# Convolution sublayer of a six-sublayer encoder: the taps' diagonal blocks are made during the feed-forward sublayer ahead of it, kept in DRAM and loaded per channel tile; taps stand amid projection tiles; weight splits are held at the convolution's head

## Chip, cores and metric

The kernel runs on one core of a Trainium2 chip. The metric is device time in microseconds of one execution, lower is better. PE is the matmul engine, DVE the vector engine, ACT the scalar engine, POOL the general-purpose engine (GpSimd), SP the engine that here issues nearly every transfer.

## What is computed

Two layers of an encoder over 256 positions and 1024 channels, all in float32. A layer is a half-weight feed-forward sublayer, a mixer, and a second half-weight feed-forward sublayer. The mixer of the first layer is a convolution module, that of the second differential attention. In the kernel the six sublayers are called a (feed-forward), b (convolution), c, d (feed-forward), e (attention), f (feed-forward). The change touches a and b:

```python
def _half_ffn(x, g_pre, g_post, w_gate, w_up, w_down):        # a, c, d, f
    h = _rmsnorm(x, g_pre)
    f = (jax.nn.silu(h @ w_gate) * (h @ w_up)) @ w_down        # 1024 -> 2816 -> 1024
    return x + 0.5 * _rmsnorm(f, g_post)

def _conformer_conv(h, w_pw1, b_pw1, w_dw, b_dw, ln_g, ln_b, w_pw2, b_pw2):   # b
    u = h @ w_pw1 + b_pw1
    u = u[..., :D_MODEL] * jax.nn.sigmoid(u[..., D_MODEL:])
    c = depthwise_conv(u, w_dw, width=31, centred) + b_dw      # one filter per channel
    c = jax.nn.silu(_layernorm(c, ln_g, ln_b))
    return c @ w_pw2 + b_pw2
```

## The kernel before, in words

**Split products.** Each weight block of 128 x 1024 values is a job with a number. SP loads it into a `raw` buffer, ACT rounds it into `wh`, DVE writes the rest into `wl` (`split_to`), and PE forms three products per pair of operands: high by high, low by high, high by low (lines 176 to 178). Five `raw` buffers turn round (`NRAW`), so the load of job n waits for the split of job n-5. `pump` issues loads and splits up to a limit; `hold(first, n)` sets that limit to job first+n, and `release` lifts it or moves it on once the instructions given to it are done.

**Sublayer a.** `ffn` goes through 22 steps `kt`. Each step is a projection tile `gua` of 48 matmuls (gate and up), an evacuation on DVE and ACT (`sga`, `hfa`, then the split pair `hha`, `hla`), and 12 matmuls of the down projection into `acca`, which use the `hha` and `hla` of the step before. PSUM has two banks for `gua`, so the tile of step kt+2 cannot start before `hfa` of step kt has been written. After the last step `conv_params` (line 590) loads the convolution's taps and biases (one transfer of 31 rows, four small ones), turns them on PE (`pp`), and splits the taps into `wdh` and `wdl`, one scalar per channel and tap.

**Sublayer b.** `lead` makes channel tiles 0 to 3 (`pxb`, turned by `py`), `projs` tiles 4 to 7 (`gub`). `glu` turns each into `u`, split into `us` (high and low). Per channel tile ct, `build(ct)` makes two blocks `dg` of 128 x 1024 on DVE, in which each channel's 32 taps stand on diagonals (line 634), and `taps(ct)` multiplies them with `us` on PE in 96 matmuls of 32 rows (line 649) into four PSUM banks `cv`. Each bank is then folded: ACT copies half of it (`ca`, line 655), DVE adds (`ta`, line 656), ACT copies (`ca`, line 657), DVE adds into `co` (line 658). `centre` shifts and squares `co`. `step(ct)` is build(ct+1), taps, centre; the dictionary at the end of `conv` says after which tile's `glu` which steps stand. The layer norm's sums, `m2`, and the Silu into `zf` and `z` follow, then the second pointwise product `accb`.

**Order.** Each engine runs its instructions in the order of its row. The framework's scheduler fixes these rows when the kernel is built, from priorities and its own estimates; an instruction at the head of a row that waits holds everything behind it on that engine. `heads` names, for each sublayer, the job up to which loads and splits are held at its end (`None` for no hold); `LEAD` is 8.

Of the kernel before, what the change touches and what calls it, by code (L numbers as in the profile page):

```python
# [9 lines left out]
F32 = mybir.dt.float32  # L10
# [32 lines left out]
WARM0 = 6  # L43

# [10 lines left out]
def trunk_kernel(  # L55
# [289 lines left out]

    def hook_flips():
        while flips:
            tc.keep_in_program_order(T.transpose(*flips.pop(0), ident))
# [34 lines left out]
    def proj(w1, w2, f, name):  # L383
# [3 lines left out]
        for n, w in enumerate((w1, w2)):  # L387
            for k in range(KD):
                hi, lo = w(k)
                mm3(ps[:, n, :], hi[:, c], lo[:, c], xTh[:, k, :], xTl[:, k, :], k == 0, k == KD - 1)  # L390
                if (n, k) == (0, KD - 1):
                    hook_flips()
        return ps
# [99 lines left out]
    def ffn(hp, jb, name, late=None):  # L493
# [27 lines left out]
        for kt, ps in projs([(c, jb[c][:2]) for c in range(2, len(jb))], name):  # L521
            c, f = divmod(kt, 2)
            if kt == 4:
# [93 lines left out]

    def conv(hp, name):
# [11 lines left out]
        def build(ct):  # L630

            dgs[ct] = [big(f"dg{ct}{n}", F32R) for n in range(2)]
            for dg, w in zip(dgs[ct], (wdh, wdl)):
                V.tensor_tensor(dg.rearrange("p (t c) -> p t c", c=STRIP),
                                same.unsqueeze(1).to_broadcast([P, TAPS, STRIP]),
                                r32(w)[:, ct, :].unsqueeze(2).to_broadcast([P, TAPS, STRIP]), ALU.mult)

        def taps(ct):
# [6 lines left out]
            for j in range(TAPS // NPH):  # L645
                for n, (d, u) in enumerate(((dh, uh), (dl, uh), (dh, ul))):
# [13 lines left out]
        def centre(ct):  # L660
            c = co[ct]
            V.scalar_tensor_tensor(c, c, par[:, 16 + ct:17 + ct], shift, ALU.add, ALU.subtract)
            sqs[ct] = hp.tile([P, S], F32, tag="sq", name=f"sq{ct}", bufs=2)
            A.activation(sqs[ct], c, AF.Square)

        def lead():
            tm = [big(f"tm{tb}", F32).rearrange("p (i c) -> p i c", c=2 * FC) for tb in range(NTB)]
            for tb, i, ps in proj_x(JC1[:2], TWO, name):
                A.copy(tm[tb][:, i, :], ps)
                if tb == 0:  # L670
                    continue
                for f in range(2):
                    ps = ps_mi.tile([P, 2, S], F32, tag="mi", name=f"py{i}{f}")
                    for n in range(2):
                        for b in range(NTB):
                            T.transpose(ps[:, n, b * P:(b + 1) * P],
                                        tm[b][:, i, n * FC + f * P:n * FC + (f + 1) * P], ident)
# [47 lines left out]
        hold(J01[0][0].ids[0], 0)  # L725
        build(0)
        for ct, ps in lead():
# [12 lines left out]
            for n in {2: (0,), 3: (1,), 4: (2, 3), 5: (4,), 6: (5,), 7: (6, 7)}.get(ct, ()):  # L740
                step(n)
        A.activation(warm, par[:, 0:1], AF.Silu)
# [66 lines left out]
    def attn(hp, name):  # L809
# [115 lines left out]
        ("a", lambda p: ffn(p, J00, "a", late), ffn_norm_pre[0, 0], ffn_norm_post[0, 0], True, conv_params),  # L925
# [8 lines left out]
    heads = [None] + [jb[0][0].ids[0] for jb in (J01, J10)] + [None, J11[0][0].ids[0]]  # L934
# [52 lines left out]
```

## Time and profile before

| what | value |
|---|---|
| median of three runs | 1037.87 us (1035.88 to 1038.41) |
| the profiled execution | 1037.48 us |
| its span, first to last instruction | 1035.7 us |
| PE busy | 1010.0 us, 98% of the span |
| DVE busy | 653.1 us, 63% |
| ACT busy | 538.0 us, 52% |
| POOL busy | 50.7 us, 5% |
| transfers | 177.14 MB, of which 1.05 MB written |

The profile is of one execution. Its own time is 0.39 us under the median, and 1.8 us of it lie outside the span. The busy time of PE counts a matmul until its modelled end, so full busy time is not full speed; the granted clock of PE stands beside it as a share of 2.4 GHz. A line number belongs to the kernel before; in the kernel after, the same code stands some lines lower (L455 for L450, L545 for L538, L679 for L656).

### The profile page before, as it was taken

The numbers are of one execution on the slowest core, as the hardware profiler recorded it, in microseconds if no ns is written. First come the engines' busy times: TensorE is split into PE (matmuls) and PEld (weight loads), VectorE is DVE, ScalarE is ACT, GpSimd is POOL, SyncE is SP. The second block draws the span as 40 slices with busy tenths as digits, with TensorE's granted clock in tenths as the row PEclk, the third lists the DMA queues.
The fourth block names the chain that finished last, engine by engine and source line by source line (L and its number), as shares of the span: only waits on it lengthen the run. The fifth ranks groups of instructions, "written<-read, shape, count | busy, mean of one in ns | idle before, by whom it ended". The sixth has DMA issues, their size and how long they took to land.

```text
span 1035.7 us, 18641 instructions
## 1 busy us (share of the span) xinstructions
PE 1010.0 (98%) x7576; PEld 932.5 (90%) x7576; DVE 653.1 (63%) x993; ACT 538.0 (52%) x877; POOL 50.7 (5%) x92
## 2 busy tenths in 40 slices
PE   8999999988989999999999999999999999999997
PEld 7999999888887989999899999998899789999995
DVE  5775667688777584646477646556778667645542
ACT  6654544465457373535346535445578556535431
POOL 0000000031410000000000000001000100000000
PEclk9999999999899999999999999999999999999999
DMA  7887555371220585655537756563752237765511
GB/s 244 278 280 227 172 184 193 116 247 48 84 83 11 184 294 184 193 174 184 162 122 251 239 181 196 182 198 123 258 163 84 80 103 233 238 200 171 186 51 41
DMA packets 130366, 177.14 MB, mean 171 GB/s; under 512 B 6165, under 2 KB 112709, under 8 KB 130280
## 3 DMA queue, kind: packets, MB, share of 16 engines
q1 hardware_dynamic: 130280, 175.95, 52.8%
q8 instruction: 59, 0.97, 0.4%
q14 instruction: 27, 0.22, 0.1%
HBM read 174.88 MB, written 1.05 MB: 170 GB/s over the span
## 4 chain that ended last, share of the span: by engine, by line
PE 86%; DVE 5%; ACT 3%; issue 2%; DMA 1%; POOL 1%; SPq 0%; DVEq 0%; POOLq 0%; ACTq 0%
PE guf L177 3%; PE guc L177 3%; PE guc L176 3%; PE gua L177 3%; PE gud L178 3%; PE gud L176 3%; PE gua L178 3%; PE gua L176 3%; PE guf L176 3%; PE gud L177 3%; PE guf L178 3%; PE guc L178 3%; PE pxa L429 2%; PE cv L649 2%; PE accf L177 2%
## 5 line engine op out<-in xcount | busy, mean ns | idle before, releaser
L450 DVE TENSOR_TENSOR wl<-raw,wh 128x1024 fp32r<-128x1024 f32 x314 | 380.9, 1225 | 101.6 <-ACT wh L450 98.5
L450 ACT CAST wh<-raw 128x1024 fp32r<-128x1024 f32 x314 | 325.7, 1051 | 107.8 <-PE guc L177 11.6
L176 PE MATMUL gud<-xTh,wh 128*128 128x256 f32 x288 | 81.0, 281 | 0.0
L176 PE MATMUL gua<-xTh,wh 128*128 128x256 f32 x288 | 81.0, 281 | 0.0
L176 PE MATMUL guf<-xTh,wh 128*128 128x256 f32 x288 | 81.0, 281 | 0.0
L176 PE MATMUL guc<-xTh,wh 128*128 128x256 f32 x288 | 81.0, 281 | 0.0
L177 PE MATMUL gua<-xTl,wh 128*128 128x256 f32 x288 | 80.9, 281 | 0.0
L177 PE MATMUL guc<-xTl,wh 128*128 128x256 f32 x288 | 80.9, 281 | 0.0
L177 PE MATMUL guf<-xTl,wh 128*128 128x256 f32 x288 | 80.9, 281 | 0.0
L177 PE MATMUL gud<-xTl,wh 128*128 128x256 f32 x288 | 80.9, 281 | 0.0
L178 PE MATMUL guf<-xTh,wl 128*128 128x256 f32 x288 | 80.9, 281 | 0.0
L178 PE MATMUL guc<-xTh,wl 128*128 128x256 f32 x288 | 80.9, 281 | 0.0
L178 PE MATMUL gua<-xTh,wl 128*128 128x256 f32 x288 | 80.9, 281 | 0.0
L178 PE MATMUL gud<-xTh,wl 128*128 128x256 f32 x288 | 80.9, 281 | 0.0
L176 PEld LDWEIGHTS guf<-xTh,wh 128*128 128x128 f32 x288 | 54.3, 189 | 0.5
L176 PEld LDWEIGHTS guc<-xTh,wh 128*128 128x128 f32 x288 | 54.3, 189 | 0.5
L176 PEld LDWEIGHTS gud<-xTh,wh 128*128 128x128 f32 x288 | 54.3, 189 | 0.5
L176 PEld LDWEIGHTS gua<-xTh,wh 128*128 128x128 f32 x288 | 54.3, 189 | 0.5
L177 PEld LDWEIGHTS gud<-xTl,wh 128*128 128x128 f32 x288 | 54.3, 189 | 0.5
L177 PEld LDWEIGHTS guc<-xTl,wh 128*128 128x128 f32 x288 | 54.3, 188 | 0.5
L177 PEld LDWEIGHTS guf<-xTl,wh 128*128 128x128 f32 x288 | 54.3, 188 | 0.5
L177 PEld LDWEIGHTS gua<-xTl,wh 128*128 128x128 f32 x288 | 54.3, 188 | 0.5
(371 smaller groups left out, 2508.8 us busy)
## 6 DMA issues: line engine op xcount, KB each, us to landing
raw<-in_ffn_w_gate_dram SPq DMA_DIRECT2D x88, 512.0 KB, 4.9
raw<-in_ffn_w_up_dram SPq DMA_DIRECT2D x88, 512.0 KB, 5.0
raw<-in_ffn_w_down_dram SPq DMA_DIRECT2D x88, 512.0 KB, 4.7
raw<-in_conv_w_pw_dram SPq DMA_DIRECT2D x24, 512.0 KB, 4.6
raw<-in_attn_w_qkv_dram SPq DMA_DIRECT2D x24, 512.0 KB, 5.3
raw<-in_attn_w_o_dram SPq DMA_DIRECT2D x8, 512.0 KB, 4.3
gpre<-in_ffn_norm_pre_dram SPq DMA_DIRECT2D x3, 512.0 KB
x<-in_x_dram SPq DMA_DIRECT2D x2, 512.0 KB, 3.4
```

The lines of the kernel that those rows point to most:

```text
L176: T.matmul(o, sh, mh, start=first, stop=False)
L177: T.matmul(o, sh, ml, start=False, stop=False)
L178: T.matmul(o, sl, mh, start=False, stop=last)
L429: pin(T.matmul(ps[:, m * FC:(m + 1) * FC], s[:, k, c], w(k)[v], start=n + k == 0, stop=n == 2 and k == KD - 1))
L450: return A.copy(hi, src), V.tensor_tensor(lo, src, r32(hi), ALU.subtract)
L649: T.matmul(bank[r][:, 0:N], d[q, j * P:(j + 1) * P], u[q, NPH * j:NPH * j + N], start=j + n == 0, stop=(j, n) == (TAPS // NPH - 1, 2))
```

## The change

- `conv_params` runs inside sublayer a, at step 5, in place of its end. `diagonals`, called at each step of a, then makes the 16 blocks that `build` made before (now called `dm`, two buffers of 512 KB in turn), one per step in program order. Each is written to a DRAM buffer `kept` by a transfer that POOL issues, 512 KB each, 8.4 MB in all.
- `build(ct)` loads two blocks from `kept` by SP in place of making them on DVE.
- `taps` takes its 96 matmuls in the order high by high, high by low, low by high, each over all eight tap groups; before, the three stood together per tap group.
- step(1) and step(4) stand amid a projection tile (`mids`, run after its first 24 matmuls); step(0) stands after tile 2, step(2) after tile 4, step(3) after 5, step(5) after 6, steps 6 and 7 after 7.
- Splits are held at the end of a to the first eight jobs of the convolution and released by the lead's copies `tm`. At the end of b, `hold` is gone from the start of conv, and `centre(7)` releases the next splits on.
- The copies `tm` are grouped by i in place of tb.

```diff
+DIAG0 = 5
@@ proj
                 if (n, k) == (0, KD - 1):
                     hook_flips()
+                    while mids:
+                        mids.pop(0)()
@@ ffn
+            if aside is not None:
+                aside(hp, kt)
@@
+    def diagonals(hp, kt):
+        if kt == DIAG0:
+            with after(fetched[LATER]):
+                conv_params()
+        ct, n = divmod(kt - DIAG0 - 1, 2)
+        if kt <= DIAG0 or ct >= KD:
+            return
+        dg = hp.tile([P, 1024], F32R, tag="dg", name=f"dm{ct}{n}", bufs=2)
+        V.tensor_tensor(dg.rearrange("p (t c) -> p t c", c=STRIP),
+                        same.unsqueeze(1).to_broadcast([P, TAPS, STRIP]),
+                        r32((wdh, wdl)[n])[:, ct, :].unsqueeze(2).to_broadcast([P, TAPS, STRIP]), ALU.mult)
+        kept[ct, n] = dram.tile([P, 1024], F32, name=f"kept{ct}{n}")
+        G.dma_start(kept[ct, n], r32(dg))
@@ build
-            for dg, w in zip(dgs[ct], (wdh, wdl)):
-                V.tensor_tensor(dg.rearrange("p (t c) -> p t c", c=STRIP),
...
+            for n in range(2):
+                nc.sync.dma_start(r32(dgs[ct][n]), kept[ct, n])
@@ taps
-            for j in range(TAPS // NPH):
-                for n, (d, u) in enumerate(((dh, uh), (dl, uh), (dh, ul))):
+            for n, (d, u) in enumerate(((dh, uh), (dh, ul), (dl, uh))):
+                for j in range(TAPS // NPH):
@@ centre
+            if ct == KD - 1:
+                release(J01[0][0].ids[0], *done)
@@ lead
+            for m, (tb, i, ps) in enumerate(proj_x(JC1[:2], TWO, name)):
+                release((j0 + LEAD, j0 + LEAD + 2, j0 + LEAD + 4, j1 + 6)[m], A.copy(tm[i][:, tb, :], ps))
@@ conv
-        hold(J01[0][0].ids[0], 0)
-            for n in {2: (0,), 3: (1,), 4: (2, 3), 5: (4,), 6: (5,), 7: (6, 7)}.get(ct, ()):
+            for n in {2: (0,), 4: (2,), 5: (3,), 6: (5,), 7: (6, 7)}.get(ct, ()):
                 step(n)
+            mids.extend({3: [lambda: step(1)], 5: [lambda: step(4)]}.get(ct, []))
@@ subs, heads
-        ("a", lambda p: ffn(p, J00, "a", late), ffn_norm_pre[0, 0], ffn_norm_post[0, 0], True, conv_params),
+        ("a", lambda p: ffn(p, J00, "a", late, diagonals), ffn_norm_pre[0, 0], ffn_norm_post[0, 0], True, None),
-    heads = [None] + [jb[0][0].ids[0] for jb in (J01, J10)] + [None, J11[0][0].ids[0]]
+    heads = [jb[0][0].ids[0] for jb in (JC1, J01, J10)] + [None, J11[0][0].ids[0]]
```

What the rows look like after, at three places. In the names, the number behind the last underscore is the buffer's.

**PE, sublayer a, the down matmuls after the tile of step 5.** Before (`acca11` is the last of the four accumulators):

```order
L176 MATMUL acca11_537<-wh16_512,hha2_610 128x512
L177 MATMUL acca11_537<-wl16_513,hha2_610 128x512
L178 MATMUL acca11_537<-wh16_512,hla2_611 128x512
L176 MATMUL gua6_785<-xTh_99,wh18_524 128x256
L177 MATMUL gua6_785<-xTl_100,wh18_524 128x256
```

After:

```order
L177 MATMUL acca11_539<-wh16_514,hha2_612 128x512
L612 MATMUL pp_771<-ident_79,wdw_r_764 128x31 x8
L178 MATMUL acca11_539<-wl16_515,hha2_612 128x512
L179 MATMUL acca11_539<-wh16_514,hla2_613 128x512
L177 MATMUL gua6_817<-xTh_99,wh18_526 128x256
```

The eight transposes of the taps `wdw_r`, which stood at the end of a, now stand among these matmuls; the transpose of `par_r` follows ten matmuls into `gua6`.

**DVE, sublayer a, steps 9 and 10.** Before:

```order
L450 TENSOR_TENSOR wl39_1108<-raw39_1105,wh39_1107 128x1024
L538 TENSOR_TENSOR sga9_1111<-gua9_1038,row_602 128x256
L805 TENSOR_SCALAR lam_106<-le0_8203,le1_8211 128x1
L540 TENSOR_TENSOR sga9_1111<-sga9_1111,row_602 128x256
L542 TENSOR_TENSOR hfa9_1115<-gua9_1038,sga9_1111 128x256
L450 TENSOR_TENSOR wl40_1134<-raw40_1131,wh40_1133 128x1024
L450 TENSOR_TENSOR hla4_1017<-hfa9_1115,hha4_1016 128x256
L538 TENSOR_TENSOR sga10_1186<-gua10_1137,row_602 128x256
```

After:

```order
L455 TENSOR_TENSOR wl39_1152<-raw39_1149,wh39_1151 128x1024
L545 TENSOR_TENSOR sga9_1159<-gua9_1082,row_604 128x256
L638 TENSOR_TENSOR dm50_1768<-same_105,wdh_103 128x1024
L455 TENSOR_TENSOR wl40_1182<-raw40_1179,wh40_1181 128x1024
L638 TENSOR_TENSOR dm51_1855<-same_105,wdl_104 128x1024
L547 TENSOR_TENSOR sga9_1159<-sga9_1159,row_604 128x256
L828 TENSOR_REDUCE le1_8277<-lp1_8275 128x1
L549 TENSOR_TENSOR hfa9_1163<-gua9_1082,sga9_1159 128x256
L833 TENSOR_SCALAR subg_109<-subg_109 128x1
L638 TENSOR_TENSOR dm60_1916<-same_105,wdh_103 128x1024
L545 TENSOR_TENSOR sga10_1238<-gua10_1185,row_604 128x256
L455 TENSOR_TENSOR hla4_1061<-hfa9_1163,hha4_1060 128x256
```

Three builds now stand between `sga9` and `hla4`, the evacuation of step 9. All 16 builds stand in DVE's row between the evacuations of steps 5 and 11; each but the first two waits for the write of the build two places ahead of it. On PE the first four matmuls of `gua11` stand ahead of the 12 down matmuls after `gua10`.

**ACT, sublayer b, ahead of the first fold of channel tile 0.** Before:

```order
L450 CAST wh83_2587<-raw83_2585 128x1024
L450 CAST us00_2527<-u0_2529 128x256
L450 CAST us10_2544<-u1_2546 128x256
L450 CAST wh84_2617<-raw84_2615 128x1024
L450 CAST wh85_2623<-raw85_2621 128x1024
L669 COPY tm1_2331<-pxb11_2554 128x512
L683 ACTIVATE sgb2_2633<-py10_2628,par_102 128x256
L450 CAST us20_2635<-u2_2637 128x256
L655 COPY ca00_2750<-cv00_2649 64x257
```

After:

```order
L455 CAST wh82_2672<-raw82_2670 128x1024
L709 ACTIVATE sgb2_2699<-py10_2694,par_102 128x256
L455 CAST wh83_2678<-raw83_2676 128x1024
L455 CAST wh84_2684<-raw84_2682 128x1024
L455 CAST us20_2701<-u2_2703 128x256
L455 CAST wh85_2690<-raw85_2688 128x1024
L678 COPY ca00_2816<-cv00_2715 64x257
```

The casts of jobs 83 to 85 (weights of the second pointwise product) stood ahead of the copy `tm1` before; now they stand behind it and among the last rows ahead of the first copy out of channel tile 0's banks, `ca00`. The load of job 83 is issued behind the split of job 78, those of 84 and 85 behind the splits of 79 and 80.

## Rows read from the trace of the kernel before

**Rows 1.** The page: busy time of PE and of its weight loads, others

```profile
PE 1010.0 (98%) x7576; PEld 932.5 (90%) x7576; DVE 653.1 (63%) x993; ACT 538.0 (52%) x877; POOL 50.7 (5%) x92
```

**Rows 2.** What PE waited for, 202 to 243.4: sum, times, longest

```profile
PE pxb L178 <- DVE xTl L358: 1.2, 1, 1.2
PE cv L649 <- DVE ta L656: 1.0, 2, 0.7
PE ptb L354 <- DVE xnb L216: 0.9, 1, 0.9
PE py L676 <- ACT tm L669: 0.7, 1, 0.7
PE cv L649 <- DVE us L450: 0.5, 1, 0.5
```

**Rows 3.** The same view, 243.4 to 313

```profile
PE cv L649 <- DVE ta L656: 4.4, 5, 1.6
PE cv L649 <- DVE us L450: 1.4, 1, 1.4
PE pm L703 <- ACT e L702: 0.8, 1, 0.8
```

**Rows 4.** Stretches: length, busy by engine; last: PE clock, DMA share, GB/s

```profile
50.00:75.00 25.00, 25.00 (x177) 23.32 (x176) 18.49 (x23) 14.98 (x18) 0.00 (x0) 1.00 0.85 288
...
250.00:275.00 25.00, 23.57 (x357) 22.03 (x357) 19.63 (x32) 13.38 (x30) 6.38 (x12) 0.93 0.29 83
275.00:300.00 25.00, 20.54 (x321) 19.30 (x323) 21.79 (x38) 14.52 (x32) 10.22 (x11) 0.88 0.32 89
```

**Rows 5.** Timeline of SP in sublayer a: start, length, queue, line

```profile
54.74 0.37 SPq L122 DMA_DIRECT2D raw<-in_ffn_w_up_dram  x1
...
65.34 0.35 SPq L598 DMA_DIRECT2D wdw_r<-in_conv_w_dw_dram  x1
```

**Rows 6.** The page: size and median from issue to landing of transfers

```profile
raw<-in_ffn_w_up_dram SPq DMA_DIRECT2D x88, 512.0 KB, 5.0
...
raw<-in_conv_w_pw_dram SPq DMA_DIRECT2D x24, 512.0 KB, 4.6
...
x<-in_x_dram SPq DMA_DIRECT2D x2, 512.0 KB, 3.4
...
gposta<-in_ffn_norm_post_dram SPq DMA_DIRECT2D x1, 512.0 KB, 9.0
```

**Rows 7.** Timeline of PE in sublayer a: down matmuls of steps 5, 8, 10

```profile
60.98 0.39 PE L177 MATMUL acca<-wl,hha 128*128 128x512 f32 x1
...
84.14 0.39 PE L176 MATMUL acca<-wh,hha 128*128 128x512 f32 x1
...
101.13 0.39 PE L176 MATMUL acca<-wh,hha 128*128 128x512 f32 x1
```

**Rows 8.** Timeline of DVE at the head of the convolution

```profile
214.13 1.21 DVE L634 TENSOR_TENSOR dg<-same,wdh 128x1024 fp32r<-128x1024 f32 x1
215.26 1.21 DVE L634 TENSOR_TENSOR dg<-same,wdl 128x1024 fp32r<-128x1024 f32 x1
216.40 1.28 DVE L358 TENSOR_TENSOR xTl<-ptb,xTh 128x512 fp32r<-128x512 f32 x2
```

**Rows 9.** Timeline of POOL at the head of the convolution

```profile
212.07 0.19 POOL L688 CAST us<-zero 128x15 fp32r<-128x15 f32 x1
...
213.07 1.19 POOL L688 CAST us<-zero 128x15 fp32r<-128x15 f32 x1
```

**Rows 10.** Timeline of DVE: channel tiles 0 and 1 of `u`

```profile
227.77 0.88 DVE L690 SCALAR_TENSOR_TENSOR u<-py,par,sgb 128x256 f32<-128x256 f32 x2 [0.55 <-ACT sgb L683]
```

**Rows 11.** Timeline of PE: end of channel tile 1's taps

```profile
243.50 0.70 PE L703 MATMUL pm<-e,ones_d 128*128 128x256 f32 x2
```

**Rows 12.** Timeline of ACT at the convolution's end

```profile
306.89 1.28 ACT L771 ACT_TABLE_LOAD   x1
311.90 0.88 ACT L771 ACTIVATE zf<-co,par 128x128 f32<-128x128 f32 x2 [3.73 <-DVE co L769]
```

More of the change, by code (lines that the diff above doesn't have):

```diff
@@ L344, in flip @@
         flips.append((dst, src))
+    mids = []
     def hook_flips():
@@ L491, in trunk_kernel, with ffn @@
     TWO = [(tb, i) for tb in range(NTB) for i in range(2)]
-    def ffn(hp, jb, name, late=None):
+    def ffn(hp, jb, name, late=None, aside=None):
         q = []
@@ L616, in conv_params @@
         tmp.__exit__(None, None, None)
+    dram = ctx.enter_context(tc.tile_pool(name="dram", bufs=1, space=bass.MemoryType.DRAM))
+    kept = {}
+    def diagonals(hp, kt):
[11 more added lines that the diff above has]
+        G.dma_start(kept[ct, n], r32(dg))
     def conv(hp, name):
@@ L632, in build @@
             dgs[ct] = [big(f"dg{ct}{n}", F32R) for n in range(2)]
-            for dg, w in zip(dgs[ct], (wdh, wdl)):
-                V.tensor_tensor(dg.rearrange("p (t c) -> p t c", c=STRIP),
-                                same.unsqueeze(1).to_broadcast([P, TAPS, STRIP]),
-                                r32(w)[:, ct, :].unsqueeze(2).to_broadcast([P, TAPS, STRIP]), ALU.mult)
+            for n in range(2):
+                nc.sync.dma_start(r32(dgs[ct][n]), kept[ct, n])
         def taps(ct):
@@ L661, in centre @@
             c = co[ct]
-            V.scalar_tensor_tensor(c, c, par[:, 16 + ct:17 + ct], shift, ALU.add, ALU.subtract)
+            done = [V.scalar_tensor_tensor(c, c, par[:, 16 + ct:17 + ct], shift, ALU.add, ALU.subtract)]
             sqs[ct] = hp.tile([P, S], F32, tag="sq", name=f"sq{ct}", bufs=2)
-            A.activation(sqs[ct], c, AF.Square)
+            done.append(A.activation(sqs[ct], c, AF.Square))
+            if ct == KD - 1:
+                release(J01[0][0].ids[0], *done)
         def lead():
-            tm = [big(f"tm{tb}", F32).rearrange("p (i c) -> p i c", c=2 * FC) for tb in range(NTB)]
-            for tb, i, ps in proj_x(JC1[:2], TWO, name):
-                A.copy(tm[tb][:, i, :], ps)
+            tm = [big(f"tm{i}", F32).rearrange("p (b c) -> p b c", c=2 * FC) for i in range(2)]
+            j0, j1 = JC1[0][0].ids[0], JC2[0].ids[0]
+            for m, (tb, i, ps) in enumerate(proj_x(JC1[:2], TWO, name)):
+                release((j0 + LEAD, j0 + LEAD + 2, j0 + LEAD + 4, j1 + 6)[m], A.copy(tm[i][:, tb, :], ps))
                 if tb == 0:
@@ L676, in lead @@
                             T.transpose(ps[:, n, b * P:(b + 1) * P],
-                                        tm[b][:, i, n * FC + f * P:n * FC + (f + 1) * P], ident)
+                                        tm[i][:, b, n * FC + f * P:n * FC + (f + 1) * P], ident)
                     yield 2 * i + f, ps
```

## Prediction

> **What bounds the kernel now.** I read the page first: PE is busy for 98% of the span [rows 1], so time is to be had only where PE waits or its clock is low, and is lost wherever PE is made to wait. Then the list of what PE waited for, over the convolution alone. Up to the end of channel tile 1's taps (243.5 [rows 11]) it waited 4.3 us [rows 2]: 2.1 at the head for the normed input (`xnb`, `xTl`), the rest for `us`, `tm` and `ta`. From there to the end of the stage it waited 6.6 us [rows 3], nearly all on DVE's `ta` and `us`. Then the table by stretches: PE's mean clock is 0.93 from 250 to 275 and 0.88 from 275 to 300 [rows 4]; against full clock that is 0.07 x 25 + 0.12 x 25 = 4.8 us. It fell, each time, amid taps and behind such waits. So the convolution offers at most 4.3 + 6.6 + 4.8 = 15.7 us. Sublayer a offers nothing: PE is busy for all 25 us of 50 to 75 at clock 1.00 [rows 4], so everything that the change puts there has to fit beside it, and the transfer engines there are 0.85 busy already [rows 4].
>
> **The taps' parameters in a.** The eight transposes cost the same wherever they stand; new is that they stand where PE passes at 60.98 [rows 7], while their load is issued behind a weight load that went out at 54.74 [rows 5], so at about 55.1. The row of before has no landing for that load. Bounds from its neighbours: 3.4 us for a lone large load, 9.0 for one issued among the same small ones [rows 6]. That gives a wait of none (55.1 + 3.4 is before 60.98) to 64.1 - 61.0 = 3.1 us. It is 31 rows in a saturated stretch, so I take 7.9, nearer to 9.0: it lands at 63.0, and **PE waits 2.0 us**. The small loads come behind it, and their transpose stands ten matmuls later: no further wait.
>
> **The 16 builds and their writes in a.** On DVE one build takes 1.13 us from start to start [rows 8], as long as a weight split; 16 are 18 us, and DVE is free for 6.5 of 25 us there [rows 4], so by busy time alone they fit into the 50 us in which DVE's order puts them. What decides is the wait: two buffers, so each build waits until the write of the build two ahead has landed. Call L the time from a build's end to the landing of its write. No write of this size and no transfer issued by POOL is in the trace. Bounds: 3.4 us (a lone load) and 9.0 (the slow neighbour) [rows 6]; loads of the same size in their queue take 5.0 at the median [rows 6]. POOL has to issue it while DVE is busy, and POOL's small copies take 0.19 us alone and 1.19 beside DVE's builds [rows 9]; half of that for the issue makes **L = 5.6**.
>
> Now down DVE's order by hand. PE resumes at 63.0, `par_r` is turned 1.5 us later, copy, cast and subtraction follow in series: the first build starts at about 66.8. On its buffer a build comes every 1.13 + 5.6 = 6.73 us at best: 66.8, 73.5, 80.3, 87.0. The one at 87.0 (dm30) stands ahead of the low half `hla` of step 7, which is then written at 88.7; PE came to its use at 84.14 [rows 7] + 2.0, third matmul 86.6: it waits 2.1. After that dm31 waits until 90.8, dm40 follows step 8's evacuation at 94.1, dm41 waits until 97.5, then four splits stand ahead of step 9's evacuation (to 103.4), and with dm50, one split and dm51 between its parts `hfa` is written at 108.2. PE ended `gua10` at 101.13 [rows 7] + 2.0 + 2.1 = 105.2, and the first matmuls of `gua11` need the bank that `hfa` frees: 3.0. dm60 waits for dm50's write (104.9 + 5.6 = 110.5), and `hla` of step 9 stands behind it, written at 112.4 where PE would use it at 109.6: 2.8. Steps 10 to 12 add 0.4. Sum **8.3 us**. The same walk with L = 3.4 gives 0.7, with 4.0 2.1, with 5.0 5.2, with 7.0 16.7 and with 9.0 28.8: about 2 us per us of L at first, 6 beyond 5.5. Weights don't run short by it: the splits keep their order, and on the bus 8.4 MB at the 288 GB/s that ran at 0.85 [rows 4] is some 25 us of a whole bus, which the spare 0.15 and later more carries in about twice the builds' 50 us only if loads are pushed back; they are issued far ahead, so I count nothing for it but put it into the upper bounds of L.
>
> The Trainium skill weighs here, in "DMA: Bandwidth & Descriptors", section on the anatomy of a transfer on the GpSimd path: 2.0 us plus the bytes at 436 GB/s, so 3.2 us for 512 KB as an estimate from that page. By it the walk would give under 0.7 us and the whole sum about 7.6 less than mine. The nearest row, 5.0 for loads in a queue [rows 6], speaks for more than that.
>
> **The convolution's head, to the end of channel tile 1.** Builds and splits no longer stand ahead of `xTl`: the two builds and what was behind them in [rows 8] go, and the 2.1 us of waits for `xnb` and `xTl` [rows 2] with them. `u` of tiles 0 and 1 then stands at 227.8 - 2.1 = 225.7 [rows 10], tile 0's taps end near 230.6, and 24 matmuls of `gub4` run to 233.5. But now the casts of jobs 83 to 85 stand on ACT ahead of tile 0's fold, and their loads are issued behind the splits of 78 to 80, which follow `us` at 229.4, 230.5 and 231.7. With 4.6 us each [rows 6] the last lands at 236.3, the fold starts at 237.4, and four banks are folded far enough at 239.9, so tile 1's taps wait 6.4 us and end at 242.8. Before they ended at 243.5 [rows 11] with 16 matmuls of `gub4` done in place of 24 (0.95 us). The gain is 0.7 + 0.95 = **1.7 us** out of the 4.3 that were to be had; loads of 3.4 us make it 2.9, of 5.5 us 0.8.
>
> **Channel tiles 2 to 7.** DVE has no builds and no splits of the next sublayer among its folds; the blocks come by SP, each asked for when the taps two tiles before have ended, some 9 us ahead, against 4.6 to land [rows 6]: no wait. Of the 6.6 us [rows 3] I keep 0.8 for `pm`, 1.2 where tile 7's taps follow tile 6's without cover (the first fold), and 1.0 for steps that now have 24 matmuls between taps and not 48: 3.6 us gained. Of the clock's 4.8 us I take half, 2.4, since the waits that stood ahead of each fall go, but the taps themselves keep PE as lightly loaded as before; the bounds are none and all. Together **6.0 us**, from 2.6 to 9.4.
>
> **The convolution's end.** Five casts now stand between the last square and the Silu's table load (306.89 [rows 12]), and two splits of DVE ahead of `m2`. ACT idles 3.7 us before `zf` [rows 12], which hides most: 5 x 1 us less 3.7 is 1.3, one more cast waits for a load issued behind a split. I take **2.0 us lost**, from 0.5 to 4. The order of the 96 matmuls costs nothing by itself: same count, same shapes, banks all started in the first group as before.
>
> **Sum.** +2.0 +8.3 -1.7 -6.0 +2.0 = +4.6 us on the profiled 1037.5, which is 0.4 under the median of the runs: **1042.1 us**. The convolution alone wins 5.7; sublayer a pays 10.3 for it.
>
> **Rivals.** First, **the writes land fast** (faster): if L is 4.0 or less, a pays 2.0 + 2.1, and a clock that stays full and a tile 1 that waits less give 9.4 + 2.9 - 2.0 in the convolution: -6.2, **1031.3**. It decides at L of about 4.4, where a's stalls (3.3) and 2.0 for the parameters equal the convolution's 5.7 within half a microsecond. For it: a lone load lands in 3.4. Against: the bus is 0.85 busy there, and two writes may be under way at once. Chance 0.2.
> Second, **middle writes**: L of 4.4 to 5.2, stalls 3.3 to 6.2, net -0.4 to +2.5, **1038.5**. For it: the median of 5.0 with nothing added for POOL. Chance 0.25.
> Third, **POOL's issue starves**: what POOL does beside DVE's two-input operations takes six times as long [rows 9], and in this stretch DVE is hardly ever idle. If each write is held for one or two DVE operations, L is 7 to 9: stalls 16.7 to 28.8, net +13 to +25, **1050 to 1063**. The Trainium skill says so of transfers issued by GpSimd, in "SBUF — State Buffer", section on the two sides of SBUF: their descriptors are written through a port pair that DVE can lock, and issuing from SP or ACT avoids it. Our rows show the lock on POOL's copies alone; no run here shows it on a transfer. Chance 0.2.
>
> **Chances and range.** The forecast (L of 5.2 to 6.6, 1040 to 1048) has 0.35, 0.05 of it within the bound. A difference under 0.3% (3.1 us) can't be told from none here. Faster by more: 0.2, all from the first rival. Within: 0.25 + 0.05 = 0.3. Slower: 0.3 + 0.2 = 0.5. The range leaves out half of the first and most of the upper half of the third: 1031 to 1054.
>
> **What would show it.** Right: PE's waits between 84 and 115 on `hla` and `hfa`, DVE idle ahead of L638 put down to the writes, landings of `kept` between 5 and 7 us; one wait of about 2 us on the load of `wdw_r`; a wait of some 6 us at tile 1's taps behind ACT's casts; no wait on DVE's builds after that, clock above 0.93 in 250 to 300. Wrong: landings under 4.4 us and no wait in a, or DVE early enough that the folds of steps 7 and 9 stand clear of the builds, or a clock that falls just as often.

## The result and the profile after

The changed kernel takes 1048.05 us (median of 5 runs, 1045.55 to 1051.04) against 1037.87 of the kernel before (5 runs, 1035.88 to 1039.48). The ratio is 1.0098, with a 95% interval from 1.0074 to 1.0123: slower by about 10 us, or 1%. The forecast was 1042.1, with a range from 1031 to 1054. The profiled execution of after took 1051.04 us, with a span of 1049.3; it is the slowest of the five, so the profiles differ by 13.6 us where the medians differ by 10.2. Of these 13.6, 2.7 are in sublayer e, which the change doesn't touch: a gap at its head, which is between 0.4 and 2.6 us long in kernels that leave e alone, and one short stretch of low clock. Without them the profiles differ by 10.9.

I split the difference at three marks on PE: the first matmul of `pxb` (the convolution starts), the last tap `cv`, and the last matmul of sublayer b (`accb`).

| stretch of PE | before, us | after, us | difference | forecast |
|---|---|---|---|---|
| to the first `pxb` | 202.0 | 221.1 | +19.1 | +10.3 |
| first `pxb` to the end of tile 1's taps | 41.5 | 46.4 | +4.9 (+4.0 without the 8 extra `gub` matmuls, 0.95 us) | -1.7 |
| from there to the last tap | 58.3 | 43.4 | -14.9 (-14.0 without those 8) | -6.0 |
| last tap to the last `accb` | 35.7 | 37.4 | +1.7 | +2.0 |
| sublayers c, d | | | 0 | 0 |
| sublayer e | | | +2.7 | 0 |

The parts are further off than the sum: sublayer a loses 8.8 us more than forecast, the stretch to the end of tile 1's taps 5.7 more, and the stretch behind it gains 8.0 more. The larger gain hides more than half of the larger losses.

The page of after: busy time (answers [rows 1]), the chain's shares, the queue of POOL's writes, and the landing of the new transfers (size, median us from issue to landing).

```profile
PE 1010.9 (96%) x7576; PEld 931.1 (89%) x7576; DVE 650.6 (62%) x993; ACT 539.7 (51%) x879; POOL 46.8 (4%) x108
...
q0 software_dynamic: 2304, 8.39, 2.1%
...
PE 83%; DMA 6%; DVE 4%; issue 3%; ACT 3%; POOL 1%; SPq 0%; DVEq 0%; POOLq 0%; ACTq 0%
...
kept<-dm POOLq DMA_DIRECT2D x16, 512.0 KB, 4.9
dg<-kept SPq DMA_DIRECT2D x16, 512.0 KB, 3.2
```

PE's busy time is nearly what it was; the span has grown around it, and 6% of the chain is now DMA (1% before). What PE waited for from 40 to 130, where before its row of matmuls had no such gap (us in total, times, longest):

```profile
PE pp L612 <- DMA wdw_r<-in_conv_w_dw_dram: 4.9, 1, 4.9
PE acca L179 <- DVE hla L455: 3.7, 1, 3.7
PE gua L177 <- DVE subg L833: 2.7, 1, 2.7
PE acca L177 <- ACT hha L455: 1.8, 1, 1.8
```

The first is the transpose of the taps, which waits for its load. The other three are the evacuations of steps 7 and 9, which stand behind builds in DVE's row: 3.7 + 2.7 + 1.8 = 8.2 us. In all 13.1 us of waits. The clock explains 5.6 of the remaining 6.0, half of the time that PE was busy in three stretches at low clock. The table by stretches shows them (length, busy time and count of PE, PEld, DVE, ACT, POOL; then granted clock, DMA share, GB/s), first in sublayer a, then around the convolution's tile 1:

```profile
63.36:70.19 6.83, 4.34 (x21) 3.89 (x21) 0.51 (x2) 0.40 (x1) 0.00 (x0) 0.50 0.61 206
94.08:97.49 3.41, 3.41 (x8) 2.22 (x8) 0.75 (x2) 0.00 (x0) 0.53 (x1) 0.50 0.83 304
121.38:124.79 3.41, 3.41 (x11) 2.73 (x10) 2.86 (x4) 0.36 (x1) 0.53 (x1) 0.50 0.73 285
257.92:268.16 10.24, 7.32 (x99) 6.68 (x99) 5.02 (x12) 4.42 (x12) 0.00 (x0) 0.50 0.95 364
268.16:312.00 43.84, 42.71 (x757) 40.39 (x755) 28.82 (x66) 26.09 (x67) 9.07 (x22) 1.00 0.42 137
```

The granted clock is 0.50, the lower of the two levels (1.2 of 2.4 GHz), during or just after each wait: during the one at 60.99 to 65.85, after those at 92.05 and at 117.24. Matmuls in such a stretch take about twice as long: in the one at 94.08 those of the down projection start 0.43 us apart, and 0.23 behind its end. The rows of after that answer to the first of [rows 4], and the one behind it:

```profile
50.00:75.00 25.00, 20.14 (x131) 18.29 (x130) 16.00 (x21) 10.14 (x14) 1.28 (x2) 0.86 0.70 233
75.00:100.00 25.00, 23.20 (x146) 20.50 (x145) 17.28 (x22) 7.90 (x11) 2.82 (x6) 0.93 0.97 329
```

From 50 to 75 the clock fell from 1.00 to 0.86 and PE from 25.00 us busy to 20.14.

The convolution shows the same in both directions. What PE waited for from 240 to 320 in after (answers [rows 2] and [rows 3]):

```profile
PE cv L672 <- issue: 5.6, 1, 5.6
PE cv L672 <- DVE ta L679: 2.1, 2, 1.5
PE pm L729 <- ACT e L728: 0.5, 1, 0.5
```

5.6 and 1.5 of these are the wait ahead of tile 1's taps (from 253.82 to 261.71 with two matmuls between). `issue` means that the profile names nothing that ended the first of them; the rows of DVE, under the third experiment, show what stood there. What is left for tiles 2 to 7 is two gaps of 0.6 and 0.5 us, where [rows 3] had 6.6. The same stretch of work in the two kernels, tile 1's end to the last tap, before and then after:

```profile
243.50:301.80 58.30, 51.60 (x758) 48.10 (x757) 47.86 (x82) 32.49 (x73) 16.60 (x22) 0.91 0.26 74
```

```profile
267.50:310.90 43.40, 42.27 (x750) 39.91 (x749) 28.80 (x65) 25.86 (x66) 9.07 (x22) 0.99 0.44 144
```

PE runs the same matmuls (8 fewer) in 43.4 us instead of 58.3: DVE has 19 us less to do, the clock stays at full from 268.16 on, 0.7 us behind the start of this stretch, and PE is busy for 42.3 of the 43.4 us.

### The profile page after: what moved, and what is told of

It reads as the page before. It is cut to its first block, busy times and chain, and to the rows that moved or that the text cites. A ratio compares the mean times of both kernels' runs of the same rounds, so it can differ in the third digit from the quotient of the medians.

```text
span 1049.3 us, 18714 instructions
## 1 busy us (share of the span) xinstructions
PE 1010.9 (96%) x7576; PEld 931.1 (89%) x7576; DVE 650.6 (62%) x993; ACT 539.7 (51%) x879; POOL 46.8 (4%) x108
## 4 chain that ended last, share of the span: by engine, by line
PE 83%; DMA 6%; DVE 4%; issue 3%; ACT 3%; POOL 1%; SPq 0%; DVEq 0%; POOLq 0%; ACTq 0%
PE guf L178 3%; PE guc L178 3%; PE gud L178 3%; PE gud L179 3%; PE guc L177 3%; PE gud L177 3%; PE guf L179 3%; PE guc L179 3%; PE guf L177 3%; PE cv L672 2%; PE gua L177 2%; PE gua L178 2%; PE gua L179 2%; PE pxa L434 2%; PE accf L179 2%
## 5 line engine op out<-in xcount | busy, mean ns | idle before, releaser
L455 ACT CAST wh<-raw 128x1024 fp32r<-128x1024 f32 x314 | 324.7, 1051 | 112.2 <-PE gud L178 11.6
L179 PEld LDWEIGHTS gua<-xTh,wl 128*128 128x128 f32 x288 | 54.9, 191 | 0.1
```

The costliest lines, as they stand in the source:

```text
L179: T.matmul(o, sl, mh, start=False, stop=last)
L455: return A.copy(hi, src), V.tensor_tensor(lo, src, r32(hi), ALU.subtract)
```

## The experiments

The theory after the result, A: the loss in sublayer a is one chain, in which two buffers for the builds and some 5 us for a write make DVE wait, what stands behind the builds in DVE's row comes late, PE waits, and the clock falls behind each wait; beside it stand a wait for the parameters and a wait at tile 1. Rivals: the traffic of the writes and loads itself (B), the builds' DVE time (C), POOL as the engine that issues (D, the third rival of the prediction), the new order of the 96 tap matmuls (E). In the quoted expectations A is this theory and E this rival; B, C and D can stand for a rival of that run alone, which is spelled out there. Each ratio is to the kernel before, measured beside that run (medians of 1036.4 to 1037.9 us).

**Four buffers for the builds.** The bytes, the issuing engine and the number of builds stay.

```diff
-        dg = hp.tile([P, 1024], F32R, tag="dg", name=f"dm{ct}{n}", bufs=2)
+        dg = hp.tile([P, 1024], F32R, tag="dg", name=f"dm{ct}{n}", bufs=4)
```

> The changed kernel with four buffers for the blocks in sublayer a in place of two, nothing else. If the waits of builds for their writes are what costs there (theory A), PE's waits of 1.8, 2.7 and 3.7 us after the tiles of steps 8 and 10 go, and with them two of the clock's falls to 1.2 GHz of 3.41 us each (1.7 us each): 8.2 + 3.4 = 11.6 us less than the changed kernel, near 1037 us. If it is the traffic itself (theory B: 8.4 MB written on a bus that is 0.97 busy, weights late) or DVE's added work, the waits only move, and under 5 us are won: 1043 or more.

1037.28 us, ratio to the kernel before 0.9987 (0.9970 to 1.0004): 10.8 us below after. The builds' line, in after and then in this kernel (what DVE's idle time before them ended on: us, times):

```profile
L638 DVE TENSOR_TENSOR dm<-same,wdl x8: 1214/1218/1226, 72.8 to 132.3; 128x1024 fp32r<-128x1024 f32 x8
...
  DMA kept<-dm: 11.8, 7
```

```profile
L638 DVE TENSOR_TENSOR dm<-same,wdl x8: 1215/1218/1226, 73.1 to 114.4; 128x1024 fp32r<-128x1024 f32 x8
...
  DMA kept<-dm: 0.4, 1
```

DVE's idle time for the writes fell from 11.8 us to 0.4, and the builds end 18 us earlier. PE's waits on the evacuations fell from 8.2 to 0.6 us, and from 75 to 125 the clock is full:

```profile
75.00:100.00 25.00, 24.38 (x168) 22.20 (x168) 23.29 (x30) 11.32 (x15) 4.98 (x10) 1.00 1.01 353
100.00:125.00 25.00, 25.00 (x178) 23.37 (x177) 21.38 (x31) 13.31 (x18) 2.67 (x5) 1.00 0.98 360
```

The bus is fuller than in after, and a write lands in 6.4 us at the median, slower than after's 4.9. So neither the traffic (B) nor the builds' DVE time (C) costs PE more than 0.6 us of waits here, and the landing time isn't the cause by itself: what costs is landing time against two buffers. DVE's row moved in this run too, since the scheduler put the builds closer together once it had four buffers; that makes DVE's work among the evacuations denser, not lighter. The first `pxb` is still 8.3 us late, by the 5.2 us wait for the parameters and the low clock beside it.

**The parameters loaded one step earlier and turned one step later.**

```diff
-        if kt == DIAG0:
+        if kt == DIAG0 - 1:
             with after(fetched[LATER]):
-                conv_params()
+                conv_loads()
+        if kt == DIAG0 + 1:
+            conv_params()
```

> The changed kernel with the taps' parameters loaded one step earlier in sublayer a (step 4) and turned on PE one step later (step 6). Theory A: the wait of 4.9 us for the load goes, with the stretch of 6.83 us at 1.2 GHz behind it (some 2 to 3 us of work): 7 us less than the changed kernel, near 1041. Theory B (the load of 31 rows starves on the busy bus wherever it is asked for): the wait stays within 2 us of what it was, 1046 or more.

1041.53 us, ratio 1.0032 (1.0016 to 1.0049): 6.5 us below after. The wait for the load is gone, and with it the low clock from 63.36. The waits for the writes are still there:

```profile
PE acca L177 <- ACT hha L455: 5.2, 2, 2.8
PE acca L179 <- DVE hla L455: 2.5, 2, 2.2
```

7.7 us against 8.2. So the two losses in a are separate, and each cost more than its wait: some 5.4 us of waits came off, and the first `pxb` comes 6.8 us earlier. The clock is low twice behind the remaining waits, for 3.41 us from 89.75 and for 6.83 from 110.23.

**Tile 1's wait taken away.** Jobs 82 to 87 (second pointwise weights) are let go behind the fold of tile 1 and no longer ahead of tile 0's.

```diff
-                release((j0 + LEAD, j0 + LEAD + 2, j0 + LEAD + 4, j1 + 6)[m], A.copy(tm[i][:, tb, :], ps))
+                release((j0 + LEAD, j0 + LEAD + 2, j0 + LEAD + 4, j1)[m], A.copy(tm[i][:, tb, :], ps))
...
+            if ct == 1:
+                release(JC2[0].ids[0] + 6, *done)
```

> The changed kernel with jobs 82 to 87 released behind the fold of channel tile 1, so that ACT's casts of 82 to 85 no longer stand ahead of the fold of tile 0. Theory A: the waits of 5.6 and 1.5 us ahead of tile 1's taps go, and with them the stretch of 10.24 us at 1.2 GHz (some 3 to 4 us of work); up to 1.5 us come back where a block of tile 1 lands late: 8 to 10 us less than the changed kernel, near 1039. Theory C (the wait is for the blocks loaded by SP, not for the casts): the wait stays, under 3 us won.

1044.12 us, ratio 1.0055 (1.0030 to 1.0081): 3.9 us below after, some 5 less than expected. In after, ACT's row ahead of tile 1's taps reads as forecast: casts that wait for their loads, then the first copies `ca` out of tile 0's banks at 257.51 (start, length, [idle before, releaser]).

```profile
252.66 1.05 ACT L455 CAST wh<-raw 128x1024 fp32r<-128x1024 f32 x1 [0.69 <-DMA raw<-in_conv_w_pw_dram]
255.17 1.04 ACT L455 CAST wh<-raw 128x1024 fp32r<-128x1024 f32 x1 [1.47 <-DMA raw<-in_conv_w_pw_dram]
256.12 0.40 ACT L455 CAST us<-u 128x256 fp32r<-128x256 f32 x1
256.44 1.05 ACT L455 CAST wh<-raw 128x1024 fp32r<-128x1024 f32 x1
257.51 0.64 ACT L678 COPY ca<-cv 64x257 f32<-64x257 f32 x2
```

DVE's first two `ta` follow behind a split, and PE goes on behind the first of them, at 259.38:

```profile
258.87 0.74 DVE L679 TENSOR_TENSOR ta<-cv,ca 64x257 f32<-64x257 f32 x2
```

```profile
259.38 0.86 PE L672 MATMUL cv<-us,dg 32*128 32x260 f32 x2 [5.56 <-issue]
```

With the casts held, tile 1's taps waited 0.44 + 1.81 us and no longer 5.6 + 1.5. But six casts let go at one point stood together behind tile 1's fold, ahead of `e`, the copies of `co` that PE sums into `pm`, and PE waited there instead:

```profile
PE pm L731 <- ACT e L730: 3.2, 1, 3.2
PE cv L672 <- DVE ta L679: 2.4, 2, 1.8
```

The casts are the cause of tile 1's wait, and letting them all go later moves half of it.

**The convolution of after, with the blocks built on DVE in it and nothing in a.** No writes, no loads; the new places of steps, splits and taps stay.

```diff
-            for n in range(2):
-                nc.sync.dma_start(r32(dgs[ct][n]), kept[ct, n])
+            for dg, w in zip(dgs[ct], (wdh, wdl)):
+                V.tensor_tensor(dg.rearrange("p (t c) -> p t c", c=STRIP),
...
-        ("a", lambda p: ffn(p, J00, "a", late, diagonals), ffn_norm_pre[0, 0], ffn_norm_post[0, 0], True, None),
+        ("a", lambda p: ffn(p, J00, "a", late), ffn_norm_pre[0, 0], ffn_norm_post[0, 0], True, conv_params),
```

> The changed kernel with the blocks made on DVE in the convolution as before, no writes and no loads of them, parameters at the end of sublayer a again; held splits, places of the taps and the order of their matmuls stay as changed. Sublayer a is then as before (19 us less in the profile). Theory A (the convolution gains because the builds are off DVE there): folds stand behind builds again, and the convolution takes about as long as before or longer, with the wait at tile 1 on top: 1036 to 1044. Theory D (it gains by the places of the taps and the held splits): the convolution keeps its 10 us, near 1029.

1035.52 us, ratio 0.9970 (0.9953 to 0.9988), between what the two theories gave. Sublayer a is as before (first `pxb` at 202.2). The convolution, first `pxb` to last tap, takes 96.4 us; before 99.8, after 89.8. So of the 10.0 us that after wins there, 3.4 come from the new places, the wait at tile 1 included, and 6.6 from taking the builds off DVE. What PE waited for in it shows why:

```profile
PE cv L674 <- DVE ta L681: 9.6, 6, 5.7
```

**The other half: the blocks written in a and loaded, the convolution's places as before.**

```diff
+    def diagonals(hp, kt):
...
-            for dg, w in zip(dgs[ct], (wdh, wdl)):
...
+            for n in range(2):
+                nc.sync.dma_start(r32(dgs[ct][n]), kept[ct, n])
...
+        ("a", lambda p: ffn(p, J00, "a", late, diagonals), ffn_norm_pre[0, 0], ffn_norm_post[0, 0], True, None),
```

> The kernel before with only the blocks moved: parameters and builds in sublayer a with two buffers and writes as in the change, loads in the convolution; places of the taps, order of matmuls, held splits and releases as before. Sublayer a loses its 17 to 19 us as in the changed kernel. Theory A: with the builds off DVE the convolution gains some 7 to 9 us even at the old places, and there is no wait for casts at tile 1: 1045 to 1049. If the loads help only at the new places (theory D), the convolution gains under 3 us: 1052 or more.

1050.26 us, ratio 1.0105 (1.0079 to 1.0131). Sublayer a ends 20.1 us later than before, with the same waits as in after; the convolution takes 93.4 us, so loads alone win 6.4 of after's 10.0, in agreement with the run above.

```profile
PE pp L608 <- DMA wdw_r<-in_conv_w_dw_dram: 5.4, 1, 5.4
PE acca L179 <- DVE hla L451: 3.8, 3, 2.7
PE gua L177 <- DVE subg L827: 3.2, 1, 3.2
PE acca L177 <- ACT hha L451: 0.9, 1, 0.9
...
PE cv L669 <- DMA dg<-kept: 2.3, 1, 2.3
```

The last line is new: here one load of blocks came late for its taps. It doesn't occur in after.

**The old order of the 96 tap matmuls.**

```diff
-            for n, (d, u) in enumerate(((dh, uh), (dh, ul), (dl, uh))):
-                for j in range(TAPS // NPH):
+            for j in range(TAPS // NPH):
+                for n, (d, u) in enumerate(((dh, uh), (dl, uh), (dh, ul))):
```

> The changed kernel with the 96 matmuls of a channel tile in the order of before (the three products together per tap group). Tiles 2 to 7 gained 14 us in the profile where waits and clock explain some 10. If the order of the matmuls gives the rest (theory E), this kernel is 3 to 5 us slower than the changed one, 1051 to 1053. If the order costs nothing, as the prediction had it, it is within 1.5 us of 1048.

1047.21 us, ratio 1.0084 (1.0065 to 1.0104): the interval covers after's 1.0098. From tile 1's end to the last tap it takes 43.2 us, after 43.3. The order costs nothing that this run can tell; E falls.

**The writes issued by SP.** This asks rival D.

```diff
-        G.dma_start(kept[ct, n], r32(dg))
+        nc.sync.dma_start(kept[ct, n], r32(dg))
```

> The changed kernel with the 16 writes issued by SP in place of POOL, in the row of the weight loads. If POOL's issue is what makes a write slow, builds wait less and the three waits in sublayer a (8.2 us) fall by more than half: 1042 or less. If the busy bus sets the landing (theory A: from build to landing 0.3 us for the issue, 4.9 for the transfer), the waits stay within 3 us, and loads behind a write that waits for its build may add some: 1045 to 1052.

1036.35 us, ratio 0.9997 (0.9981 to 1.0013). The time is the one that the rival gave, but not by its mechanism. The page's line for the writes:

```profile
kept<-dm SPq DMA_DIRECT2D x16, 512.0 KB, 5.0
```

The median of 5.0 us, against 4.9 from POOL, stands on two of the 16 writes (5.4 and 4.6), the only ones whose landing the profile tells. The packed trace has more, though no view prints it: 16 semaphore updates per write, the signals that the waiting engine counts. They put the last update of all 16 writes between 3.0 and 7.9 us behind the issue, 6.1 at the median; POOL's took 2.9 to 8.0. So the writes land no faster. SP also issued them later: up to 6.5 us behind the build, between weight loads in its row. What moved is DVE's order: with the issue on another engine the scheduler put the builds at other places, over 75 us of DVE's row and not 60, so that fewer of them meet a write that is still under way:

```profile
L638 DVE TENSOR_TENSOR dm<-same,wdl x8: 1215/1217/1225, 72.9 to 146.9; 128x1024 fp32r<-128x1024 f32 x8
...
  DMA kept<-dm: 5.0, 2
```

PE's waits behind the builds fell from 8.2 to 0.9 us, while the wait for the parameters (4.7 us) and the one at tile 1 (5.4 + 1.5) stayed. And in after POOL doesn't hold its writes back: the builds end at 72.91 and 74.05, and its issues start 0.3 us later.

```profile
73.22 0.74 POOL L642 DMA_DIRECT2D kept<-dm  x1 [52.69 <-DVE dm L638]
74.36 0.54 POOL L642 DMA_DIRECT2D kept<-dm  x1 [0.40 <-DVE dm L638]
```

So D falls, and A is sharpened: what counts is how far apart the builds stand against the time of a write on two buffers. As a test of the engine alone the run is spoilt, since the order moved with it; that verdict rests on the landing times and on POOL's prompt issues.

**All three repairs together.** Four buffers, the parameters early, and jobs 82 to 87 let go two by two behind the squares of tiles 1, 2 and 3. On top of the edits of the first two runs, with the release in `lead` ending at `j1` as in the third:

```diff
+            if ct in {1: 2, 2: 4, 3: 6}:
+                release(JC2[0].ids[0] + {1: 2, 2: 4, 3: 6}[ct], *done)
```

> The three mends together: four buffers in sublayer a, parameters loaded at step 4 and turned at step 6, and jobs 82 to 87 released two by two behind the squares of channel tiles 1, 2 and 3. Theory A (each wait is a cause of its own, and the low clock follows waits): sublayer a as before within 2 us, the convolution 18 to 20 us shorter than before, its end 1.6 us longer: 1019 to 1024. Theory B (the waits are one shortage that moves from place to place): over 1030.

1033.30 us, ratio 0.9952 (0.9936 to 0.9969): faster than the kernel before, but 9 to 14 us above what I expected by adding up the savings. It is the time that this run's theory B gave, one shortage that moves from place to place. The first `pxb` is at 206.6, still 4.5 later than before, with five waits of 0.3 to 1.1 us behind the evacuations. The convolution takes 87.0 us: it had taken 89.8, and of tile 1's 7.0 us of waits 2.2 are left. But 1.1 us of wait is new at tile 4, where casts now stand, and the clock fell at 242.55 and at 269.86.

**The same, with the next sublayer's splits let go behind tile 5 and not at the last square.**

```diff
-            if ct in {1: 2, 2: 4, 3: 6}:
-                release(JC2[0].ids[0] + {1: 2, 2: 4, 3: 6}[ct], *done)
-            if ct == KD - 1:
-                release(J01[0][0].ids[0], *done)
+            if ct in {1: 2, 2: 4, 3: 6, 5: 8}:
+                release(JC2[0].ids[0] + {1: 2, 2: 4, 3: 6, 5: 8}[ct], *done)
```

> As best1, and jobs 88 and 89 released behind the square of channel tile 5, with no release at the last square, so that five casts and two splits leave the place ahead of the layer norm's Silu. If they cost the 1.5 us at the end of the convolution, 1 to 2 us less than best1; if their splits now stand ahead of the folds of tiles 6 and 7 and hold PE there, as in the kernel before, 1 to 3 us more.

1034.07 us, ratio 0.9965 (0.9948 to 0.9981); the interval covers that of the run before. The convolution's end got its 1.7 us back (last tap to last `accb` 35.7 us, as in the kernel before), and tile 7 pays for it: the casts stand among its folds.

```profile
PE cv L680 <- DVE ta L687: 3.7, 1, 3.7
PE cv L680 <- issue: 0.8, 1, 0.8
```

**Builds on DVE in the convolution, with the staged release.** What could be had without writes and loads: the release two by two, on the kernel that builds on DVE and does nothing in a.

```diff
+            if ct in {1: 2, 2: 4, 3: 6}:
+                release(JC2[0].ids[0] + {1: 2, 2: 4, 3: 6}[ct], *done)
```

> The convolution as changed with blocks made on DVE there, nothing in sublayer a (conv_dve), and jobs 82 to 87 released two by two behind the squares of tiles 1, 2 and 3. If the wait for the casts at tile 1 is what the held splits cost, 5 to 7 us less than conv_dve: 1029 to 1031, and less than best1, so that the blocks' way through DRAM wins nothing over making them in place. If builds on DVE then hold the folds, 1033 or more.

1037.03 us, ratio 1.0003 (0.9991 to 1.0016). It doesn't get faster: with casts and splits among the tiles the folds wait for DVE.

```profile
PE cv L674 <- DVE ta L681: 10.3, 7, 3.1
```

With this release, then, blocks made elsewhere are worth 0.5%, once a doesn't pay for them (0.9952 against 1.0003). Against the better kernel with builds on DVE, the one without the staged release (0.9970, 0.9953 to 0.9988), the interval of the three repairs overlaps; only the last run below is clear of it, and its place for tile 1 was not tried with builds on DVE.

**The three repairs, with tile 1's taps behind a whole tile of projections.** Against the run of all three repairs:

```diff
-            for n in {2: (0,), 4: (2,), 5: (3,), 6: (5,), 7: (6, 7)}.get(ct, ()):
+            for n in {2: (0,), 4: (1,), 5: (3,), 6: (5,), 7: (6, 7)}.get(ct, ()):
                 step(n)
-            mids.extend({3: [lambda: step(1)], 5: [lambda: step(4)]}.get(ct, []))
+            mids.extend({4: [lambda: step(2)], 5: [lambda: step(4)]}.get(ct, []))
```

> As best1, with the taps of tile 1 behind the whole tile of gub4 (48 matmuls in place of 24) and those of tile 2 amid gub5. The wait of 1.8 us ahead of tile 1's third matmul and the stretch of 3.41 us at 1.2 GHz behind it (1.7) go: 3 us less than best1, near 1030. If the fold of tile 1 or 2 then comes late elsewhere, no gain: 1032 to 1035.

1028.53 us (1027.04 to 1029.43), ratio 0.9914 (0.9891 to 0.9937). It is 0.9% faster than the kernel before and about 1.8% faster than the change as made (0.9914 / 1.0098 = 0.982). PE's waits over the convolution, and the stretches of a and of the convolution in which after's clock fell:

```profile
PE cv L680 <- DVE ta L687: 3.6, 4, 1.1
PE pm L739 <- ACT e L738: 0.7, 1, 0.7
...
PE cv L680 <- DMA dg<-kept: 0.4, 1, 0.4
```

```profile
100.00:150.00 50.00, 48.61 (x350) 45.34 (x349) 39.76 (x58) 26.43 (x35) 3.72 (x7) 1.00 0.80 273
230.00:292.00 62.00, 56.86 (x985) 51.98 (x985) 42.72 (x86) 39.98 (x91) 13.36 (x22) 1.00 0.59 207
```

No wait is longer than 1.1 us, and the clock is at full throughout, although PE is idle for 5 of the 62 us of the second stretch. By the three marks: first `pxb` 3.7 us later than before, the convolution 85.5 us (14.3 less), its end 1.7 us longer: -8.9, against -9.0 between the profiled times.

## Why the prediction was right in sign and low in size

**The wait for the parameters: mis-sized.** The place and the cause are as forecast, one wait of the transpose on `wdw_r`. It measured 4.9 us, where I took 2.0 and gave 3.1 as the upper bound. The timeline of SP, and then that of PE, in after (start, length):

```profile
54.90 0.36 SPq L605 DMA_DIRECT2D wdw_r<-in_conv_w_dw_dram  x1
```

```profile
65.85 0.39 PE L612 MATMUL pp<-ident,wdw_r 31*128 31x31 f32 x2 [4.86 <-DMA wdw_r<-in_conv_w_dw_dram]
```

The load went out at 54.90 (forecast 55.1) and PE resumed at 65.85, so up to 10.9 us went from issue to use; my bound was the 9.0 us of a load of 512 KB that stands among small ones in another place [rows 6]. A row of another load can't be the upper end for a load of 31 rows between weight loads of 512 KB. The load's own time could be had: in the packed traces the last update of its semaphore comes 9.6 us behind the issue in before (65.34 to 74.95), 10.8 in after and 10.8 in the run that issues it a step earlier, which hides the load and doesn't shorten it. For this load the semaphore gets one such late update, for a weight load 16. Why so small a load takes so long was not tested.

**The builds' waits: the mechanism right, the size right with some luck.** Forecast 8.3 us, measured 8.2: 1.8 at step 7 (2.1 forecast), 2.7 ahead of `gua11` (3.0), 3.7 at the end of step 9 (2.8), nothing later (0.4). L was forecast at 5.6; a landing of 4.9 at the median, from 2.9 to 8.0, and 0.3 us to the issue make 5.2. The walk gave 5.2 us with 5.0 and 8.3 with 5.6, so at the measured median it gives 6.2, the upper end of the second rival; that the spread of the landings makes up the rest is not shown. The walk also began at 66.8, where the first build came at 71.7, behind the longer wait for the parameters. And at step 7 PE waited for `hha` and not for `hla`: the build that waited for a write was dm20, two before dm30. At step 9 the walk had the right instructions, `hla` behind dm60's wait for the write of dm50. The four-buffer run shows the cause: with the waits on the writes gone, these waits go.

The Trainium skill's estimate for such a write, 3.2 us by "DMA: Bandwidth & Descriptors", section on the anatomy of a transfer on the GpSimd path, doesn't hold on this bus: the sixteen landed in 2.9 to 8.0 us, 4.9 at the median, and the measurement decides.

**The clock behind the new waits: the step that failed.** I counted the waits and nothing for what follows them. Sublayer a ran at full clock before [rows 4], and I wrote that it offers nothing; I didn't ask what new waits there would do to it. Three stretches at 0.50 came with them and explain 5.6 of the 6.0 us that the waits leave of the 19.1. In the convolution the wait at tile 1, 7.0 us against the forecast 6.4, came with 10.2 us at 0.50, in which PE was busy for 7.3; at full clock that work is half, so some 3.7 us. The walk gave a gain of 1.7 us to the end of tile 1's taps; measured is a loss of 4.0. 0.6 of the 5.7 us between them is the wait's size and about 3.7 the clock; the remaining 1.4 stays unassigned. Together the clock costs that I left out are about 9.3 us, more than the miss of the whole sum (about 6).

**Tiles 2 to 7: mis-sized in the other direction.** Forecast 6.0 us, range 2.6 to 9.4; measured 14.0, well outside that range. Without this second error the time would have stood some 8 us higher, past the range's upper end of 1054; that it fell inside is luck. Waits went from 6.6 to 1.1 us, so 5.5 where I kept 3.0 and took 3.6. The clock I gave half of 4.8 us; it stayed at full throughout. Those two make 5.5 + 4.8 = 10.3 at most, so about 3.7 us of the gain were in neither of the views that I summed. The row from 243.50 to 301.80 shows where: PE was idle there for 6.7 us and its 51.6 busy us ran at 0.91. After ran 750 of the 758 matmuls in 42.3 busy us. Less 0.95 for the 8, that is 8.4 us of busy time saved, beside 5.6 us of idle time. The row's clock explains at most (1 - 0.91) x 58.3 = 5.2 of the 8.4; the other 3 us stay open, since no run separates them. They lie among the taps and not among the projections: at full clock the matmuls of `gub` start 0.125 us apart on average before and 0.123 after. The two halves of the edit tried alone show only whose gain it is: 6.4 or 6.6 us of the whole convolution's 10.0 by the loads, 3.4 by the places.

I had let half of the clock's loss stay with the argument that the taps themselves load PE lightly. The best version above refutes it: the same taps, none of them at low clock.

**The signs.** Two of the signs that I named for being right did not come: landings of `kept` between 5 and 7 us (2.9 to 8.0, 4.9 at the median), and a clock above 0.93 from 250 to 300 (0.90, all of it lost to the stretch at tile 1).

**The convolution's end: right.** Forecast +2.0, measured +1.7; the run that moved those splits got exactly these 1.7 us back.

**The order of the matmuls: right**, nothing.

**The third rival** gave 1050 to 1063 by a mechanism that isn't there, and its lower end is 2 us above the measured time: the time alone would have been a poor judge. POOL's issues started 0.3 us after each build and took 0.5 to 0.7 us, most of them while DVE was at work, and writes that SP issued landed no faster. The Trainium skill, in "SBUF — State Buffer", section on the two sides of SBUF, ties the block on GpSimd's descriptors to DVE operations in a 2-port mode; one with two inputs in SBUF blocks, by it, only a GpSimd operation that reads SBUF. The builds and weight splits here have two inputs, so this case doesn't test the rule as it stands there.

**What was still not expected in the experiments.** Savings don't add. The repairs of the write waits (10.8 us), the parameters (6.5) and tile 1 (3.9) come to 21 us on after's 1048; together they gave 14.8, and 19.5 only after tile 1's taps also got a longer cover. Each repair let the next thing in the row come late. What remains in the best version is 3.7 us in a, of which 2.3 are PE's waits on `hha` and `hla`, none longer than 1.1, and the 1.7 at the end.

## What to carry to other kernels

A DRAM write of some 5 us behind a two-deep buffer lets its producer go at about two items per 5 us, and everything behind the producer in its engine's row waits with it: count the buffers against the spacing of the items, not against the engine's free time. Every new wait of a few us on a saturated PE is to be priced with the stretch of low clock that the trace shows behind such waits, and a wait that is taken away gives that back as well. Work that is held back and then let go at one point stalls whatever stands behind that point; let go in pairs, at places with slack, it costs little.

## What the runs showed of the chip that I had not expected

- In sublayer a, where PE had run at full clock for all 25 us of 50 to 75 [rows 4], one wait of 4.9 us came with 6.83 us at 1.2 GHz, and waits of 1.8 and of 2.7 + 3.7 us with 3.41 us each. In the best version waits of up to 1.1 us, 5 us in 62, came with none, while in the run of the three repairs a fall did follow one of 1.1 us.
- A load of 31 rows, issued amid weight loads of 512 KB, took 8.7 to 11.6 us in the 13 traces, from issue to the last update of its semaphore, while loads of 512 KB took about 5 at the median [rows 6].
- A write of 512 KB lands no later from POOL's queue than from SP's (2.9 to 8.0 us and 3.0 to 7.9, by the semaphores), beside a bus that, in after, is 0.70 and 0.97 busy in the two stretches shown.
- Reading a block back takes 3.2 us at the median of the page in after and 6.2 in the best version, but these stand on two of 16 loads each. By the semaphore updates all 16 took 3.1 to 8.8 us in after and 3.5 to 9.7 in the best version; PE waited for one in the best version, 0.4 us, and for none in after.
